# Output weights scaled and split in the x, B, C stage; that stage's raw weights fetched from ScalarE's queue

## The chip, the cores and the metric

The kernel runs on one core of a Trainium2 chip. The metric is the device time of one execution in microseconds (us), and lower is better. One execution of the kernel before was also recorded by the hardware profiler; the rows below come from that record. The engines are named PE (TensorE, matmul), DVE (VectorE), ACT (ScalarE), POOL (GpSimd) and SP (SyncE, which only issues DMAs here). ACT issues DMAs too, from a queue of its own.

## The reference

One layer of a diffusion backbone over 2048 latent tokens and 256 context tokens of width 1024. After an adaptive RMS norm, one wide projection feeds two mixers, and one output projection joins them:

```python
mod = silu(c) @ w_ada + b_ada                     # shift, scale, and the gate g of width 1024
p   = (rmsnorm(h, norm_w) * (1 + scale) + shift) @ w_in
u_pool, z_pool, z_ssd, xbc, dt = split(p)         # xbc: x, B and C of the state-space mixer
y_pool = (box means of u_pool - u_pool) @ pool_w * pool_scale * silu(z_pool)
y_ssd  = rmsnorm_by_group(ssd_bidirectional(silu(conv4(xbc)), dt) * silu(z_ssd), ssd_norm_w)
h      = h + g * (concat(y_pool, y_ssd) @ w_out)  # w_out: 2048 x 1024
out    = rmsnorm(h, final_norm_w)
```

The kernel does not multiply the output by g, pool_scale and the norm weight. It multiplies them into the 2048 rows and 1024 columns of w_out ahead of time: each raw row block of 128 rows is multiplied by `rowscale` (one number for each row) and by the gate (one number for each column). This preparation is what the change moves.

## The kernel before

**Split matmuls.** Every float32 operand is held as a high part, rounded to the format PE reads, and a low part, the rest. A product is hi*hi + hi*lo + lo*hi, so a 128x512 block of a projection over a depth of 1024 takes 24 matmuls. A raw weight tile (128x1024, 512 KB, tag `wraw`, a pool with two slots) is loaded by SP; ACT makes the high part by a CAST (L219), and POOL the low part by a subtraction (L220).

**Stages.** (1) Start, up to about 150 us: modulation, norm, and the first two column tiles of x. (2) The x, B, C stage, up to about 500 us: column tiles `ct` 2 to 15. Each has four blocks of 512 tokens, and those below 12 a context block too. A block is 24 matmuls; ACT copies the result out of PSUM (L315), POOL fills the edges of the copy (L317 to L323), DVE and ACT do the convolution of width 4 (L268 to L272), and the results go to DRAM. At the head of tile ct, `weights()` loads and splits the weights of tile ct + 1. (3) The sweep, 502 to 813 us: z and pool projections of the upper token blocks, and the backward state sweep, one chunk at a time. (4) The box stage, 813 to 1065 us: box means on DVE beside the projections of the lower blocks. (5) The ramp, 1065 to 1150 us: the first steps of the main loop in the hand-written order of the string `RAMP`. (6) The main loop, 1150 to 1690 us: 16 steps, each with scores, state, gate, norm and the output projection against the prepared `wout`.

**Who sets the order.** A tile scheduler orders the instructions of stages 1 to 4, by a simulated timeline; each engine then works strictly in its order. The ramp and the main loop stand as written.

**The gate and w_out before.** The gate row is summed in tiles 10 to 13 by `gate_row` (128x1024 multiplications on DVE) and stored to `s_gate`. In the sweep it is read back, and two matmuls with a matrix of ones spread it over all partitions into two PSUM tiles, `gb0` and `gb1`, of the tag `pp`. That tag has four banks, which the projections of sweep and box share, and gb0 and gb1 keep two of them until their last use in the ramp. Row blocks 8 to 15 of w_out are scaled in the sweep (`rescale`: two DVE instructions each) and stored raw to `s_wo`. `prepare(k)` then loads a raw block k (512 KB), scales it if k < 8, casts the high part on ACT (L846) and subtracts the low part on POOL or DVE (L851). It runs for k = 0 to 4 in the box stage and for 5 to 15 in the ramp, where the words `prep_load/5`, `prep_hi/5` and so on give each part its place.

Of the kernel before, what the change touches and what calls it, by code (L numbers as in the profile page):

```python
# [8 lines left out]
F32 = mybir.dt.float32  # L9
F32R = mybir.dt.float32r  # L10
AF = mybir.ActivationFunctionType
ALU = mybir.AluOpType
# [11 lines left out]
def hybrid_block(ctx, tc, d, out):  # L24
    nc = tc.nc
    P = 128
# [9 lines left out]
    def pp(name):  # L36
        return psum.tile([P, 512], F32, tag="pp", name=name)

    def aux(name):
        return psum.tile([P, 512], F32, tag="aux", name=name)  # L40

    def const(name, shape, src=None, dt=F32, pool=None):
        t = (pool or cpool).tile(shape, dt, tag=name, bufs=1, name=name)
        if src is not None:
            nc.sync.dma_start(t, src)
        return t

    def dram(name, shape):
        return drp.tile(shape, F32, tag=name, name=name)

    def mm(o, l, r, start, stop):
        nc.tensor.matmul(o, l, r, start=start, stop=stop)  # L52
# [9 lines left out]
    s_zp = dram("s_zp", [8, P, 1024])  # L62
    s_yp = dram("s_yp", [NCH, P, 8, P])
    s_af = dram("s_af", [P, 2, NC2, 16])
    s_gate = dram("s_gate", [P, 1024])
    s_wo = dram("s_wo", [8, P, 1024])
    s_rows = dram("s_rows", [2, NCH, 16, P])

    wstack = ExitStack()
# [1 line left out]
    rpool = rstack.enter_context(tc.tile_pool(name="rawp", bufs=2, side="right"))  # L71
    wpool = wstack.enter_context(tc.tile_pool(name="wpool", bufs=2, side="right"))
    dstack = ExitStack()
    dp = dstack.enter_context(tc.tile_pool(name="dtp", bufs=1, side="right"))
# [3 lines left out]
    sp = start.enter_context(tc.tile_pool(name="startp", bufs=2))  # L78
# [138 lines left out]
    def split_weights(raw, nm, eng=nc.gpsimd):  # L217
        w = wpool.tile([P, 2, 8, P], F32R, tag="w", name=f"w_{nm}")
        nc.scalar.copy(w[:, 0], raw)  # L219
        eng.tensor_tensor(w[:, 1], raw, w[:, 0].bitcast(F32), op=ALU.subtract)  # L220
        return w

    def weights(src, nm):

        return split_weights(raw_weights(src, nm), nm)
# [105 lines left out]

    hc = dp.tile([P, 2, 8, 256], F32R, tag="hc", name="hc")
    dt_raw = const("dt_raw", [P, NC2, 32], pool=dp)
    wd = dp.tile([P, 8, P], F32R, tag="wd", name="wd")
    ctxt = Tokens(hc, 256, d["ctxT"], 1, "c", wpool.tile([P, 8, 256], F32, tag="w", name="xc"))
    ada = [slot(f"ada{a}", [P, 4, 2048], F32) for a in range(2)]
    cu = slot("cu", [P, 8192], F32)
# [163 lines left out]
    tabs = ctx.enter_context(tc.tile_pool(name="tabs", bufs=1))  # L501
    triU = const("triU", [P, P], d["triU"], pool=tabs)
    triL = const("triL", [P, P], d["triL"], pool=tabs)
    n4 = [P, 2, NC2, 16]
    dt_t = const("dt_t", n4, pool=tabs)
    af_t = const("af_t", n4, pool=tabs)
# [55 lines left out]
    def gate_row(k):  # L562

        wg = rpool.tile([P, 1024], F32, tag="wraw", name=f"wg{k}")
        nc.sync.dma_start(wg, d["w_ada"][k * P:(k + 1) * P, 2048:3072])
        if k == 0:
            nc.vector.tensor_scalar(gacc, wg, scol[:, k, 0:1], None, op0=ALU.mult)
        else:
            nc.vector.scalar_tensor_tensor(gacc, wg, scol[:, k, 0:1], gacc, op0=ALU.mult, op1=ALU.add)
        if k == 7:  # L570
            brow = rpool.tile([1, 1024], F32, tag="wraw", name="brow")
            nc.sync.dma_start(brow, d["b_g"])
            nc.vector.tensor_tensor(gacc[0:1, :], gacc[0:1, :], brow, op=ALU.add)
            nc.scalar.dma_start(s_gate, gacc)

    late = [lambda c=c, b=b: c.recall(b) for c in cols[0:2] for b in (4, 0, 1, 2, 3)]
    tables = dt_tables()
# [1 line left out]
    for ct in range(2, 16):  # L579
        next(tables, None)  # L580
        col = cols[ct]
        col.w = wx.pop(ct)
        if ct < 15:
            wx[ct + 1] = weights(d["w_xbc"][ct + 1], f"x{ct + 1}")
        if ct < 12:
            col.context()
            col.context_out()
        for b in range(4):
            col.block(b)
            col.block_out(b)  # L590
            col.conv()
            if ct > 12 and late:
                late.pop(0)()
        if ct in (10, 11, 12, 13):
            for k in range(2):
                gate_row(2 * ct - 20 + k)
    gstack.close()
    cstack.close()
    dstack.close()
    tabs2 = ctx.enter_context(tc.tile_pool(name="tabs2", bufs=1))  # L600
    rowscale = const("rowscale", [P, 16], d["rowscale"], pool=tabs2)
    dskip = const("dskip", [P, 16], d["d_skip"].broadcast_to([P, 16]), pool=tabs2)
    allone = const("allone", [P, P], pool=tabs2)
    nc.vector.memset(allone, 1.0)
    mcol = const("mcol", [P, 1], pool=tabs2)
    nc.vector.memset(mcol, 1.0 / 256.0)
    hst = const("hst", [P, 4, 256], pool=tabs2)
# [102 lines left out]
    with tc.tile_pool(name="sweepp", bufs=2) as bp, tc.tile_pool(name="evp", bufs=3) as ep:  # L710
        sw, silus = sweep(bp), []
        count, taken = [0], [1]
        len_sweep, len_between = 74, 7 * 3 * 2 * 8

        def between():
            count[0] += 1
            if count[0] * len_sweep >= len_between * taken[0]:
                taken[0] += 1
                next(sw, None)

        def rescale(raw, k):

            for j in range(2):
                js = raw[:, 512 * j:512 * j + 512]
                nc.vector.scalar_tensor_tensor(js, js, rowscale[:, k:k + 1], gb[j], op0=ALU.mult, op1=ALU.mult)

        upper = (2, 3)
        for j in range(8):
            w = weights(d["w_z"][j], f"z{j}_2")
            for b in upper:  # L730
                silus.append(z_block(ep, w, j, b, between if j else None))
                if j == 0 and b == 2:
                    next(sw)
            if j == 1:
                gacc = rpool.tile([P, 1024], F32, tag="wraw", name="gacc2")
                nc.sync.dma_start(gacc, s_gate)
                gb = [pp(f"gb{j}") for j in range(2)]
                for j in range(2):
                    mm(gb[j], allone, gacc[:, 512 * j:512 * j + 512], True, True)
            for k in {1: (), 7: (5, 6, 7)}.get(j, (j - 2,) if j else ()):  # L740
                raw = rpool.tile([P, 1024], F32, tag="wraw", name=f"wos{k}")
                nc.sync.dma_start(raw, d["w_out"][1024 + k * P:1152 + k * P, :])
                rescale(raw, 8 + k)
                nc.scalar.dma_start(s_wo[k], raw)
            for src, dst, fn in ((d["w_zp"][j], s_zp, AF.Silu), (s_wp[j], s_v, AF.Copy)):
                w = weights(src, f"p{j}_{fn}")
                for i, b in enumerate(upper):
                    t = ep.tile([P, 512], F32, tag="ev", name=f"e{j}_{b}_{fn}")
                    ps = pp(f"pp{j}_{b}_{fn}")
                    project(ps, w, hm[b], between if j else None)  # L750
                    nc.scalar.activation(t, ps, fn)
                    nc.scalar.dma_start(dst[j, :, 512 * i:512 * i + 512], t)
        for _ in sw:
            pass
# [77 lines left out]
    bx = slot("bx", [P, 8192], F32)  # L832
    wout = [slot("wout0", [P, 4, 2, 1024], F32R)]

    raws = {}

    def prep_load(k):
        raws[k] = rpool.tile([P, 1024], F32, tag="wraw", name=f"wor{k}")
        nc.sync.dma_start(raws[k], s_wo[k - 8] if k >= 8 else d["w_out"][k * P:(k + 1) * P, :])

    def prep_scale(k):
        if k < 8:
            rescale(raws[k], k)

    def prep_hi(k):
        nc.scalar.copy(wout[k // 4][:, k % 4, 0, :], raws[k])  # L846

    def prep_lo(k, eng=None):
        wo = wout[k // 4][:, k % 4]
        eng = eng or (nc.gpsimd if k in (1,3,4,5,7,13,15) else nc.vector)  # L850
        eng.tensor_tensor(wo[:, 1, :], raws[k], wo[:, 0, :].bitcast(F32), op=ALU.subtract)  # L851

    def prepare(k):
        prep_load(k)
        prep_scale(k)
        prep_hi(k)
        prep_lo(k)

    with tc.tile_pool(name="boxp", bufs=1) as xp:
        for i, j in enumerate(order):  # L860
# [256 lines left out]
    for i in (4, 5):  # L1117
        w = following()
# [81 lines left out]
        wout.append(slot(f"wout{len(wout)}", [P, 4, 2, 1024], F32R))  # L1200

    kp = None
    other = {f.__name__: f for f in (prep_load, prep_scale, prep_hi, prep_lo, z, zg, logs, work, more)}

    RAMP = """
    0:load prep_load/5 1:load 0:scores 0:carried 0:shift 0:mask 0:exponents prep_scale/5 1:shift 0:steps_mix
    prep_hi/5 logs 0:decay z/6/0 1:scores 1:carried zg/6/0 z/7/0 0:mix 0:from_states prep_load/6 
    0:mix2 1:mask 1:exponents 2:load prep_scale/6 1:steps_mix prep_hi/6 1:decay zg/7/0 2:scores 2:carried more  # L1210
    1:from_states 1:mix 0:outputs z/6/1 prep_lo/5 prep_load/7 0:load_pool prep_lo/6
    0:gate 2:mask prep_scale/7 1:mix2 prep_load/8 1:load_pool 0:squares 2:shift
    2:steps_mix 0:square_sum 2:exponents 1:outputs 0:norm_mm z/7/1 more work prep_hi/8 prep_hi/7 zg/6/1 prep_lo/8
    0:state prep_lo/7 3:load 2:from_states 1:gate 0:pool_hi 1:squares zg/7/1 logs 0:norm1 
    1:square_sum 0:norm2/0 1:pool_hi 2:decay 2:mix 0:pool_lo 1:pool_lo 3:scores 1:norm_mm 0:out/0/0
    0:out/0/1 1:norm1 0:norm2/1 0:norm2/2 0:norm2/3 0:diag 0:spread 2:mix2 3:mask 2:outputs 1:out/0/0 0:scale 3:carried 1:out/0/1
    0:ssd_hi 3:shift 2:state 0:ssd_lo 1:state 2:gate 3:steps_mix 2:squares 2:square_sum 3:exponents 2:norm_mm
# [99 lines left out]
```

## Time and profile before

| | us |
|---|---|
| median of 3 runs | 1691.6 (1691.33 to 1699.04) |
| the profiled execution, its own time | 1691.25 |
| span of its trace, first to last instruction | 1689.5 |
| PE busy | 1626.3 (96% of the span) |
| DVE, ACT, POOL busy | 1209.4, 768.4, 599.5 |

The profiled execution took 1691.25 us, 1.75 us more than its span, and lies 0.35 us below the median. The granted TensorE clock was 0.983 of full speed over the whole span. PE is the engine with the least idle time, so a change is felt where PE waits, or where its clock falls.

### The profile page before, as it was taken

The page shows a single profiled execution, that of the slowest core. Times are in us where ns is not written, and L with a number is a line of the kernel's source. Part 1 is how long each engine was busy: PE and PEld are TensorE (multiplying, and loading weights), DVE is VectorE, ACT ScalarE, POOL GpSimd, SP SyncE. Part 2 cuts the span into 40 slices and gives each one's busy share as a digit, 9 for nine tenths or more (in the row PEclk, how much of TensorE's full clock was granted, in tenths as well). Part 3 has the DMA queues.
Part 4 walks back from the last instruction along what each step waited for, and adds up shares of the span by engine and source line. Part 5 has one row for each costly group of instructions (what it writes and reads, how often), then busy time and mean ns, then how long its engine had stood idle before and what let it go on. Part 6 is the DMA issues. An engine that isn't in the chain of part 4 may idle for free. (4 is left out here: it accounts for less than half of the span.)

```text
span 1689.5 us, 25001 instructions
## 1 busy us (share of the span) xinstructions
PE 1626.3 (96%) x7786; PEld 1306.6 (77%) x7786; DVE 1209.4 (72%) x2514; ACT 768.4 (45%) x1841; POOL 599.5 (35%) x667
## 2 busy tenths in 40 slices
PE   8889999999999999999999989869999999999997
PEld 6668888888887887787887868757888888888886
DVE  2575755566772888886199998547788888888885
ACT  5563453433453444443212122455565556555653
POOL 1231111111223667775433334323333333333331
PEclk9989999999999999999999999989999999999999
DMA  9823333466564678878624356675666667666762
GB/s 388 283 75 100 76 74 73 93 155 155 144 137 153 203 248 252 255 249 272 207 87 150 114 184 187 188 223 184 186 194 208 195 203 199 198 208 192 194 194 83
DMA packets 315543, 302.57 MB, mean 179 GB/s; under 512 B 132626, under 2 KB 244114, under 8 KB 312851
## 3 DMA queue, kind: packets, MB, share of 16 engines
q1 hardware_dynamic: 246594, 237.27, 48.9%
q10 hardware_dynamic: 68816, 63.71, 11.3%
q8 instruction: 61, 1.00, 0.2%
q14 instruction: 72, 0.58, 0.1%
HBM read 207.28 MB, written 93.62 MB: 178 GB/s over the span
## 5 line engine op out<-in xcount | busy, mean ns | idle before, releaser
L52 PE MATMUL px<-hm,w_x 128*128 128x512 f32 x1536 | 364.8, 397 | 2.7 <-ACT hm L205 2.4
L52 PEld LDWEIGHTS px<-hm,w_x 128*128 128x128 f32 x1536 | 288.0, 188 | 73.3 <-ACT hm L205 4.1
L52 PE MATMUL po<-wout,yp 128*128 128x512 f32 x768 | 213.0, 413 | 0.0
L52 PE MATMUL po<-wout,ys 128*128 128x512 f32 x768 | 211.0, 410 | 0.0
L52 PE MATMUL pz<-hm,w_z 128*128 128x512 f32 x768 | 188.9, 398 | 0.7 <-POOL w_z L220 0.7
L270 DVE SCALAR_TENSOR_TENSOR cacc<-u,conv_w,cacc 128x512 f32<-128x512 f32 x168 | 141.5, 854 | 66.3 <-POOL u L320 47.5
L52 PEld LDWEIGHTS pz<-hm,w_z 128*128 128x128 f32 x768 | 145.0, 189 | 36.0 <-POOL w_z L220 1.1
L52 PEld LDWEIGHTS po<-wout,yp 128*128 128x128 f32 x768 | 135.9, 190 | 34.7 <-issue 10.6
L52 PEld LDWEIGHTS po<-wout,ys 128*128 128x128 f32 x768 | 136.3, 190 | 23.7
L960 POOL TENSOR_TENSOR yp<-yl,yp 128x256 fp32r<-128x256 f32 x64 | 50.3, 786 | 229.2 <-ACT yp L956 220.8
L644 DVE TENSOR_TENSOR xw<-xt,w_t 128x256 f32<-128x256 f32 x144 | 99.3, 728 | 31.5 <-POOL xr L651 17.0
L651 POOL TENSOR_TENSOR xr<-xw,xh 128x512 fp32r<-128x512 f32 x72 | 99.7, 1387 | 27.4 <-ACT xh L649 27.4
L960 POOL TENSOR_TENSOR ys<-yg,ys 128x256 fp32r<-128x256 f32 x64 | 63.1, 986 | 116.9 <-ACT ys L956 66.6
L52 PE MATMUL ivationFunctionType.Copy<-hm,ivationFunctionType.Copy 128*128 128x512 f32 x384 | 97.7, 401 | 2.3 <-POOL ivationFunctionType.Copy L220 1.7
L52 PE MATMUL pv<-hm,w_v 128*128 128x512 f32 x384 | 92.9, 402 | 5.9 <-ACT zt L795 5.9
L52 PE MATMUL ivationFunctionType.Silu<-hm,ivationFunctionType.Silu 128*128 128x512 f32 x384 | 95.9, 396 | 0.0
L649 ACT CAST xh<-xw 128x512 fp32r<-128x512 f32 x72 | 44.7, 621 | 110.0 <-DVE xw L644 48.9
L52 PE MATMUL pzp<-hm,w_q 128*128 128x512 f32 x384 | 91.3, 396 | 1.2 <-ACT va L788 1.2
L52 PEld LDWEIGHTS pv<-hm,w_v 128*128 128x128 f32 x384 | 73.6, 192 | 24.1 <-ACT zt L795 6.3
L52 PEld LDWEIGHTS ivationFunctionType.Copy<-hm,ivationFunctionType.Copy 128*128 128x128 f32 x384 | 73.1, 191 | 20.5 <-POOL ivationFunctionType.Copy L220 2.1
L52 PEld LDWEIGHTS pzp<-hm,w_q 128*128 128x128 f32 x384 | 72.0, 188 | 19.2 <-ACT va L788 1.6
L904 ACT ACTIVATE e<-e,nrb_t 128x128 f32<-128x128 f32 x256 | 81.1, 388 | 12.2 <-DMA e<-s_rows 11.9
(269 smaller groups left out, 3046.3 us busy)
## 6 DMA issues: line engine op xcount, KB each, us to landing
e<-s_rows SPq DMA_DIRECT2D x128, 256.0 KB, 5.1
s_tok<-tkw ACTq DMA_DIRECT2D x64, 256.0 KB, 3.0
bc<-s_bc SPq DMA_DIRECT2D x64, 256.0 KB, 4.3
st<-s_tok SPq DMA_DIRECT2D x64, 256.0 KB, 5.5
xt<-s_xt SPq DMA_DIRECT2D x72, 128.0 KB, 3.4
ada<-in_w_ada_dram SPq DMA_DIRECT2D x8, 1024.0 KB, 15.7
wraw_x<-in_w_xbc_dram SPq DMA_DIRECT2D x16, 512.0 KB, 4.4
s_bc<-cacc ACTq DMA_DIRECT2D x32, 256.0 KB, 3.2
```

What stands on the lines that cost most here:

```text
L52: nc.tensor.matmul(o, l, r, start=start, stop=stop)
L270: nc.vector.scalar_tensor_tensor(acc, u[:, k:k + n], conv_w[:, ct, k:k + 1], acc, op0=ALU.mult, op1=ALU.add)
L644: nc.vector.tensor_tensor(xw[:, s], h4(xt), w_t[:, s, c, 4 * g:4 * g + 4].unsqueeze(2).broadcast_to([P, 4, 64]), op=ALU.mult)
L649: nc.scalar.copy(xh, xw)
L651: nc.gpsimd.tensor_tensor(xr, xw, xh.bitcast(F32), op=ALU.subtract)
L904: nc.scalar.activation(s.e2[:, h, :], s.e2[:, h, :], AF.Identity, bias=nrb_t[:, s.c, 4 * s.g + h:4 * s.g + h + 1])
L960: nc.gpsimd.tensor_tensor(y[:, 1], src, y[:, 0].bitcast(F32), op=ALU.subtract)
```

## The change

The gate is now summed in tiles 3 to 6. Its last `gate_row` spreads it at once, through a PSUM tile of another tag, and ACT copies it back to SBUF, into `gacc`; `s_gate`, gb0 and gb1 are gone. A new function `prep(k)` is called once behind each block of tiles 8 to 11, 16 times in all. It loads the raw block k on SP (the same two `wraw` slots as the x weights use), scales it by halves of 512 columns on DVE, casts the high part of a half on ACT into a tile `wo` (one slot), subtracts the low part on POOL, and stores the half, 512 KB, on SP into a larger `s_wo`. `prepare(k)` has become one load of 1 MB. The raw weights of the next x tile are now fetched from ACT's queue instead of SP's. The steps of the preparation leave sweep, box and ramp; `rowscale` and the ones are made earlier; `wd`, 4 KB a partition, moves to another pool.

```diff
-    s_gate = dram("s_gate", [P, 1024])
-    s_wo = dram("s_wo", [8, P, 1024])
+    s_wo = dram("s_wo", [16, P, 2, 1024])
...
-            nc.scalar.dma_start(s_gate, gacc)
+            for j in range(2):
+                gb = aux(f"gb{j}")
+                mm(gb, allone, gacc[:, 512 * j:512 * j + 512], True, True)
+                nc.scalar.copy(gacc[:, 512 * j:512 * j + 512], gb)
+
+    def prep(k):
+
+        raw = rpool.tile([P, 1024], F32, tag="wraw", name=f"wos{k}")
+        nc.sync.dma_start(raw, d["w_out"][k * P:(k + 1) * P, :])
+        for j in range(2):
+            js = slice(512 * j, 512 * j + 512)
+            nc.vector.scalar_tensor_tensor(raw[:, js], raw[:, js], rowscale[:, k:k + 1], gacc[:, js],
+                                           op0=ALU.mult, op1=ALU.mult)
+            w = gp.tile([P, 2, 512], F32R, tag="wo", bufs=1, name=f"wo{k}_{j}")
+            nc.scalar.copy(w[:, 0], raw[:, js])
+            nc.gpsimd.tensor_tensor(w[:, 1], raw[:, js], w[:, 0].bitcast(F32), op=ALU.subtract)
+            nc.sync.dma_start(s_wo[k, :, :, js], w.bitcast(F32))
...
-            wx[ct + 1] = weights(d["w_xbc"][ct + 1], f"x{ct + 1}")
+            raw = rpool.tile([P, 8, P], F32, tag="wraw", name=f"wraw_x{ct + 1}")
+            nc.scalar.dma_start(raw, d["w_xbc"][ct + 1])
+            wx[ct + 1] = split_weights(raw, f"x{ct + 1}")
...
             col.conv()
+            if 8 <= ct < 12:
+                prep(4 * ct - 32 + b)
...
-        if ct in (10, 11, 12, 13):
+        if 3 <= ct < 7:
             for k in range(2):
-                gate_row(2 * ct - 20 + k)
+                gate_row(2 * ct - 6 + k)
...
     def prepare(k):
-        prep_load(k)
-        prep_scale(k)
-        prep_hi(k)
-        prep_lo(k)
+        nc.sync.dma_start(wout[k // 4][:, k % 4].bitcast(F32), s_wo[k])
...
-    0:load prep_load/5 1:load 0:scores 0:carried 0:shift 0:mask 0:exponents prep_scale/5 1:shift 0:steps_mix
+    0:load prepare/5 1:load 0:scores 0:carried 0:shift 0:mask 0:exponents 1:shift 0:steps_mix
```

ACT's order between column tiles 10 and 12, before. A name ends in a number that only tells tiles apart; `px11_3` is block 3 of tile 11, `u11_3` its copy, `cacc` the convolution, `w_x12` the split weights of tile 12:

```order
L315 COPY u10_2_3042<-px10_2_3017 128x512
L268 ACTIVATE cacc_10_8_3088<-u10_2_3042,conv_b_156,conv_w_154 128x512
L272 ACTIVATE cacc_10_4_3046<-cacc_10_4_3046 128x512
L262 DMA s_bc_69<-cacc_10_4_3046 128x4x128
L315 COPY u10_3_3083<-px10_3_3058 128x512
L219 CAST w_x12_3120<-wraw_x12_3118 128x1024
L268 ACTIVATE cacc_10_12_3100<-u10_3_3083,conv_b_156,conv_w_154 128x512
L272 ACTIVATE cacc_10_8_3088<-cacc_10_8_3088 128x512
L306 COPY uc11_3148<-pc11_3123 128x256
```

The same engine now, at the end of tile 11. `wo9_1` is the second half of row block 9; line numbers have moved by one (L314 for L315, L218 for L219), L590 is the new CAST and L603 the fetch of the raw x weights:

```order
L590 CAST wo9_1_3169<-wos9_3161 128x512
L314 COPY u11_3_3509<-px11_3_3484 128x512
L267 ACTIVATE cacc_11_12_3526<-u11_3_3509,conv_b_155,conv_w_153 128x512
L271 ACTIVATE cacc_11_8_3514<-cacc_11_8_3514 128x512
L261 DMA s_bc_69<-cacc_11_8_3514 128x4x128
L590 CAST wo10_0_3217<-wos10_3214 128x512
L271 ACTIVATE cacc_11_12_3526<-cacc_11_12_3526 128x512
L261 DMA s_bc_69<-cacc_11_12_3526 128x4x128
L590 CAST wo10_1_3222<-wos10_3214 128x512
L603 DMA wraw_x12_3292<-in_w_xbc_dram 128x1024
L590 CAST wo11_0_3283<-wos11_3280 128x512
L218 CAST w_x12_3294<-wraw_x12_3292 128x1024
```

The CAST of w_x12 has moved from the end of tile 10 to behind the last copy of tile 11, behind three more halves of w_out and behind the fetch of its raw tile. At the next tile boundary the order is alike: the copy of `u12_3` and the halves 12_1 to 14_1 stand ahead of the fetch of `wraw_x13`, and 15_0 behind it, ahead of the CAST of w_x13.

SP's order in the ramp, before (`wor` is a raw block of w_out, `yl`, `bc`, `e`, `tk` and `st` are inputs of the steps):

```order
L839 DMA wor7_9122<-in_w_out_dram 128x1024
L893 DMA yl0_0_9124<-s_yp_74 128x256
L839 DMA wor8_9135<-s_wo_77 128x1024
L893 DMA yl0_1_9137<-s_yp_74 128x256
L880 DMA bc0_3_9206<-s_bc_69 128x512
```

The same place now (a `wout` is the prepared tile of four row blocks):

```order
L838 DMA wout1_8912<-s_wo_76 128x2048
L874 DMA yl0_0_9239<-s_yp_74 128x256
L838 DMA wout2_9195<-s_wo_76 128x2048
L874 DMA yl0_1_9248<-s_yp_74 128x256
L838 DMA wout2_9195<-s_wo_76 128x2048 x3
L861 DMA bc0_3_9313<-s_bc_69 128x512
```

Five loads of 1 MB stand where two of 512 KB stood, and the inputs of the next steps are issued behind them.

## Rows read from the trace of the kernel before

**Rows 1.** The page: busy time of each engine; PE's granted clock in 40 slices.

```profile
PE 1626.3 (96%) x7786; PEld 1306.6 (77%) x7786; DVE 1209.4 (72%) x2514; ACT 768.4 (45%) x1841; POOL 599.5 (35%) x667
PEclk9989999999999999999999999989999999999999
```

**Rows 2.** Stretches: length, busy PE, PEld, DVE, ACT, POOL; clock, DMA share, GB/s.

```profile
200.00:502.00 302.00, 302.00 (x1390) 247.62 (x1390) 195.74 (x269) 136.48 (x209) 53.15 (x130) 1.00 0.54 117
502.00:813.00 311.00, 305.04 (x1286) 242.65 (x1285) 222.03 (x371) 128.21 (x280) 193.25 (x156) 0.99 0.73 233
813.00:1065.00 252.00, 244.95 (x1041) 196.38 (x1040) 205.06 (x79) 50.51 (x72) 94.97 (x59) 0.99 0.47 146
1065.00:1150.00 85.00, 64.43 (x292) 50.22 (x290) 44.08 (x104) 45.27 (x92) 26.93 (x21) 0.88 0.72 218
1150.00:1690.00 540.00, 530.63 (x2938) 429.71 (x2938) 428.65 (x1498) 308.92 (x996) 187.37 (x234) 1.00 0.64 188
376.78:402.00 25.22, 25.22 (x121) 20.91 (x120) 16.57 (x22) 9.65 (x16) 3.48 (x9) 1.00 0.68 149
0.00:50.00 50.00, 41.57 (x208) 29.00 (x208) 9.48 (x29) 24.46 (x63) 10.79 (x16) 1.00 0.97 385
```

**Rows 3.** PE's waits: line and what it waited for; us, times, longest.

```profile
PE yo L52 <- DMA st<-s_tok: 6.8, 1, 6.8
PE pv L52 <- ACT zt L795: 5.9, 1, 5.9
```

**Rows 4.** PE's timeline in the x, B, C stage: start, us, operation, count.

```profile
351.51 3.04 PE L52 MATMUL pc<-hc,w_x 128*128 128x256 f32 x24
354.39 22.55 PE L52 MATMUL px<-hm,w_x 128*128 128x512 f32 x96
376.78 3.04 PE L52 MATMUL pc<-hc,w_x 128*128 128x256 f32 x24
```

**Rows 5.** Timeline of all engines, 345 to 362 us, in column tile 10.

```profile
347.40 0.59 ACT L315 COPY u<-px 128x512 f32<-128x512 f32 x1 [0.57 <-ACT cacc L272]
348.05 0.19 POOL L320 COPY u<-u 128x1 f32<-128x1 f32 x1 [6.33 <-ACT u L315]
...
349.20 1.54 DVE L270 SCALAR_TENSOR_TENSOR cacc<-u,conv_w,cacc 128x512 f32<-128x512 f32 x2 [0.17 <-ACT cacc L268]
...
352.20 1.05 ACT L219 CAST w_x<-wraw_x 128x1024 fp32r<-128x1024 f32 x1
...
353.86 2.40 POOL L220 TENSOR_TENSOR w_x<-wraw_x,w_x 128x1024 fp32r<-128x1024 f32 x1
353.94 3.52 DVE L270 SCALAR_TENSOR_TENSOR cacc<-u,conv_w,cacc 128x512 f32<-128x512 f32 x2 [2.58 <-POOL u L320]
```

**Rows 6.** Groups of like instructions: busy us, mean ns of one; scaling: min/median/max.

```profile
L220 POOL TENSOR_TENSOR w_x<-wraw_x,w_x 128x1024 fp32r<-128x1024 f32 x12 | 29.6, 2470 | 7.0 <-ACT w_x L219 5.4 <-DMA s_bt<-u 0.8 <-DMA s_xt<-u 0.8
L651 POOL TENSOR_TENSOR xr<-xw,xh 128x512 fp32r<-128x512 f32 x72 | 99.7, 1387 | 27.4 <-ACT xh L649 27.4
L649 ACT CAST xh<-xw 128x512 fp32r<-128x512 f32 x72 | 44.7, 621 | 110.0 <-DVE xw L644 48.9
...
L725 DVE SCALAR_TENSOR_TENSOR wos<-wos,rowscale,gb x16: 733/742/750, 550.6 to 776.9; 128x512 f32<-128x512 f32 x16
```

**Rows 7.** DMAs: size of each, median us from issue to landing.

```profile
s_wo<-wos ACTq DMA_DIRECT2D x8, 512.0 KB, 3.2
...
wraw_x<-in_w_xbc_dram SPq DMA_DIRECT2D x10, 512.0 KB, 4.3
s_gate<-gacc ACTq DMA_DIRECT2D x1, 512.0 KB, 5.1
```

**Rows 8.** Groups of the preparation in the ramp, 1065 to 1150 us.

```profile
L846 ACT CAST wout<-wor 128x1024 fp32r<-128x1024 f32 x12 | 12.4, 1044 | 19.3 <-DMA wor<-s_wo 10.9 <-DVE zt L828 7.1 <-DVE wor L725 1.3
L851 POOL TENSOR_TENSOR wout<-wor,wout 128x1024 fp32r<-128x1024 f32 x5 | 12.2, 2446 | 30.9 <-ACT wout L846 30.9
```

**Rows 9.** Stretches of 5 us in the ramp; columns as in rows 2.

```profile
1100.00:1105.00 5.00, 3.59 (x17) 2.80 (x18) 0.17 (x1) 1.38 (x2) 0.00 (x0) 0.55 0.89 328
1140.00:1145.00 5.00, 2.71 (x8) 2.34 (x9) 4.36 (x18) 2.84 (x10) 1.86 (x3) 0.50 0.31 105
```

More of the change, by code (lines that the diff above doesn't have):

```diff
@@ L333, in hybrid_block @@
     dt_raw = const("dt_raw", [P, NC2, 32], pool=dp)
-    wd = dp.tile([P, 8, P], F32R, tag="wd", name="wd")
+    wd = sp.tile([P, 8, P], F32R, tag="wd", bufs=1, name="wd")
     ctxt = Tokens(hc, 256, d["ctxT"], 1, "c", wpool.tile([P, 8, 256], F32, tag="w", name="xc"))
@@ L503, in hybrid_block @@
     triL = const("triL", [P, P], d["triL"], pool=tabs)
+    rowscale = const("rowscale", [P, 16], d["rowscale"], pool=tabs)
+    allone = const("allone", [P, P], pool=tabs)
+    nc.vector.memset(allone, 1.0)
     n4 = [P, 2, NC2, 16]
@@ L600, in hybrid_block @@
     tabs2 = ctx.enter_context(tc.tile_pool(name="tabs2", bufs=1))
-    rowscale = const("rowscale", [P, 16], d["rowscale"], pool=tabs2)
     dskip = const("dskip", [P, 16], d["d_skip"].broadcast_to([P, 16]), pool=tabs2)
-    allone = const("allone", [P, P], pool=tabs2)
-    nc.vector.memset(allone, 1.0)
     mcol = const("mcol", [P, 1], pool=tabs2)
@@ L719, in between @@
                 next(sw, None)
[L721 to L725, printed above, removed]
         upper = (2, 3)
@@ L733, in hybrid_block @@
                     next(sw)
[L734 to L744, printed above, removed]
             for src, dst, fn in ((d["w_zp"][j], s_zp, AF.Silu), (s_wp[j], s_v, AF.Copy)):
@@ L833, in hybrid_block @@
     wout = [slot("wout0", [P, 4, 2, 1024], F32R)]
[L835 to L851, printed above, removed]
     def prepare(k):
-        prep_load(k)
-        prep_scale(k)
-        prep_hi(k)
-        prep_lo(k)
+        nc.sync.dma_start(wout[k // 4][:, k % 4].bitcast(F32), s_wo[k])
     with tc.tile_pool(name="boxp", bufs=1) as xp:
@@ L1202, in hybrid_block @@
     kp = None
-    other = {f.__name__: f for f in (prep_load, prep_scale, prep_hi, prep_lo, z, zg, logs, work, more)}
+    other = {f.__name__: f for f in (prepare, z, zg, logs, work, more)}
     RAMP = """
-    0:load prep_load/5 1:load 0:scores 0:carried 0:shift 0:mask 0:exponents prep_scale/5 1:shift 0:steps_mix
[L1209 to L1214, printed above, removed]
+    0:load prepare/5 1:load 0:scores 0:carried 0:shift 0:mask 0:exponents 1:shift 0:steps_mix
+    logs 0:decay z/6/0 1:scores 1:carried zg/6/0 z/7/0 0:mix 0:from_states prepare/6
+    0:mix2 1:mask 1:exponents 2:load 1:steps_mix 1:decay zg/7/0 2:scores 2:carried more
+    1:from_states 1:mix 0:outputs z/6/1 prepare/7 0:load_pool
+    0:gate 2:mask 1:mix2 prepare/8 1:load_pool 0:squares 2:shift
+    2:steps_mix 0:square_sum 2:exponents 1:outputs 0:norm_mm z/7/1 more work zg/6/1
+    0:state 3:load 2:from_states 1:gate 0:pool_hi 1:squares zg/7/1 logs 0:norm1
     1:square_sum 0:norm2/0 1:pool_hi 2:decay 2:mix 0:pool_lo 1:pool_lo 3:scores 1:norm_mm 0:out/0/0
```

## The prediction

> **What bounds the kernel now.** I read the page's busy times first: PE is busy for 1626.3 of 1689.5 us, no other engine over 1209.4, and its clock is full except at the start and in one slice near two thirds of the span [rows 1]. So only PE's idle time and that slice can be won, and every wait put before PE is lost. The windows by stage place this [rows 2]: in the x, B, C stage PE is busy for 302.0 of 302.0 us at clock 1.00, so nothing can be won there; sweep and box leave 6.0 and 7.1 us idle; the ramp leaves 85.0 − 64.4 = 20.6 us and has a clock of 0.88, which costs about 64.4 × 0.12 = 7.7 us more. The list of PE's waits shows the single ones [rows 3], and the timelines give the pace of the x, B, C stage [rows 4, 5].
>
> The change takes work from the stages with gaps and puts it into the one without. It is cheap there by busy time: ACT is busy for 136, DVE for 196 and POOL for 53 of 302 us [rows 2]. What decides is the order in which it stands, and what each piece waits for.
>
> **The new chain of halves.** The tile `wo` has one slot, so the CAST of a half must wait until the store of the half before has landed, and POOL's subtraction must lie between. The 32 halves are strictly serial. One period P is a CAST of 128x512, 0.62 us; a subtraction of 128x512, 1.39 in another place, or 1.24 as half of 2.47 for 128x1024 [rows 6]; a store of 512 KB from issue to landing; and the hand-overs, of which ACT to POOL took 0.06 (347.40 + 0.59 to 348.05) [rows 5], say 0.25 for all. This store isn't in the trace. Transfers of the same size took 3.2 (s_wo, in the sweep), 4.3 (the raw x weights, in this stage) and 5.1 us (s_gate, in this stage) [rows 7]. So P lies between 0.62 + 1.24 + 3.2 + 0.2 = 5.3 and 0.62 + 1.39 + 5.1 + 0.3 = 7.4. I take the 4.3 of this stage: 0.62 + 1.31 + 4.3 + 0.25 = **6.5 us**. The bytes themselves fit: 8 MB of loads and 16 MB of stores over some 225 us add about 107 GB/s to 149, against 385 GB/s in the first 50 us [rows 2].
>
> **Where PE waits for it.** Before, the CAST of w_x12 stood at the end of tile 10, a whole tile of 25.3 us (351.51 to 376.78) ahead of PE's need [rows 4]. Now ACT's order around it is: wo9_1, the last copy of tile 11, wo10_0, wo10_1, the fetch of wraw_x12, wo11_0, the CAST of w_x12. The fetch must find a free `wraw` slot, that of block 10, so it waits for POOL's half 10_1; ACT works in order, so everything behind it waits too.
>
> *Stall at tile 12.* wo9_1 stands ahead of the copy of the last block, about half a block (2.8 us) before PE ends tile 11. Two periods later comes wo10_1, then CAST and POOL (0.62 + 1.24 + 0.2 = 2.1), the load (4.3) and the CAST of w_x12 (1.05) [rows 5, 7]. PE waits 2P − 2.8 + 2.1 + 4.3 + 1.05 = 2P + 4.65: 17.7 us at P = 6.5; 15.3 and 19.5 at the ends.
>
> *Stall at tile 13.* The fetch of wraw_x13 stands behind 14_1, eight halves after 10_1, by the same path. Meanwhile PE has only the four blocks of tile 12, 354.39 to 376.78 = 22.4 us in tile 10 [rows 4]. It waits 8P − 22.4: 29.6 us; 20.0 and 36.8 at the ends. Behind it only block 15 is left, and tiles 14 and 15 find their raw weights in time.
>
> *Lag in tiles 7 to 11.* Here about one half stands behind each block copy on ACT, 20 in all, while a block with its share of the context comes every 25.3 / 4 = 6.3 us. Where P is longer, ACT's copies fall behind and PE waits for PSUM: 20 × (6.5 − 6.3) = 4.0 us; 0 and 22.0 at the ends.
>
> Together 51.3 us (35.3 to 78.3). To this comes the clock behind two long waits: a stretch of 5 us in the ramp that was partly idle ran at 0.55 [rows 9], which costs 2.25 us, so 4.5 for two. The additions in tiles 3 to 6 (the gate multiplications come earlier, two small matmuls) lie beside a DVE with 106 us free [rows 2] and I put them at 0.
>
> **What is won.** *Ramp:* 12 CASTs of 1.04 us, five subtractions of 2.45 us on POOL [rows 8] and others on DVE, and the scalings of 0.74 [rows 6] go; ACT's CASTs waited 10.9 us for raw loads [rows 8]. Ends: 0, if PE's gaps are those of the steps' own inputs, and 20.6 + 7.7 = 28.3, all idle time and all lost clock. One gap of 6.8 us is for `st`, an input from s_tok [rows 3], and there are others without the preparation (at 1140 DVE was busy for 4.36 of 5 us and PE for 2.71) [rows 9]. I take half, 14. The loads grow: a prepared block is 1 MB, and SP issues the next steps' inputs behind them; what is late next is therefore an input. *Box:* the wait of 5.9 us of pv for ACT's zt [rows 3] came with two PSUM banks of four; with four, and without the preparation of blocks 0 to 4, I take 6 (0 to 7.1). *Sweep:* 16 scalings of 0.74 us [rows 6] go, mostly beside PE: 1 (0 to 6.0). Together −21 (0 to −41.4).
>
> **Sum.** +51.3 + 4.5 − 21 = +34.8. The profiled execution took 1691.25 us (0.35 below the median of 1691.6), so 1691.25 + 34.8 = 1726. With every term at its end: 35.3 + 4.5 − 41.4 = −1.6 (1690), and 78.3 + 4.5 = +82.8 (1774).
>
> **Rivals.** *A, not slower (12%).* The stores land in 3.2 us or less, so that P is 5.3, and the ramp and box, rid of the preparation, give back all their idle time and clock: −1.6, that is 1690. For it: s_wo stores took 3.2 at a DMA share of 0.73, higher than here [rows 2, 7], and CASTs in the ramp waited for raw loads. Against it: the ramp's own inputs. It turns at the point where the gains exceed 2P + 4.65 + 8P − 22.4 + 4.5, which is 39.8 at P = 5.3: the ramp alone, with 28.3, can't do it.
>
> *B, POOL and DVE in each other's way (20%).* While POOL made the low half of w_x (353.86, 2.40 us), the pair of convolution instructions on DVE took 3.52 us instead of 1.54 [rows 5]. The new scaling and the convolution share the stage with 32 more subtractions. If each of those waits once for a convolution instruction, 1.54 / 2 = 0.77 us, P is 7.3: 19.3 + 36.0 + 20.0 = 75.3, and 75.3 + 4.5 − 21 = +58.8: 1750. Against it: such a collision needs both at once, and DVE is busy for only 65% of the stage [rows 2].
> The Trainium skill, page "SBUF — State Buffer", section "Who interferes with whom", says that a DVE instruction with two SBUF inputs contends with a GpSimd instruction that reads SBUF, since its second input comes through the shared read interface; the scaling now reads both gacc and the raw block from SBUF, where before it read the gate from PSUM. The stretch of 3.52 us agrees with that rule, which speaks for this rival and against the change. By the rule the sum would be this rival's, without it the forecast's.
>
> *C, the ramp gains nothing (15%).* Five loads of 1 MB stand on SP ahead of bc0_3 and the inputs behind it, where two of 512 KB stood. At the 328 GB/s of the busiest stretch [rows 9] a block of 1 MB takes 3.2 us, five 16, against 3.2 for the two: 12.8 us in which inputs queue, as much as I credit. Then 51.3 + 4.5 − 7 = +48.8: 1740. For it: the DMA share is already 0.72, and 0.89 in the stretch [rows 2, 9].
>
> **How the numbers follow.** The forecast has 53% and an own range of 1708 to 1744 (P from 6.0 to 7.0 moves the sum from 42.3 to 66.3, and the gain in the ramp by some 7 either way). With A at 1690, C at 1740 and B at 1750, a range of 1698 to 1762 leaves out most of A and the upper end of B. About 0.5%, 8.5 us, is what a measurement of this kernel tells from no change. Faster needs A with still shorter stores: 5%. Within 0.5%: the rest of A and a little of the forecast's lower end, 9%. Slower: 86%.
>
> **What would show it.** Right: in the new trace PE waits about 18 us ahead of the first matmul of tile 12 and about 30 ahead of tile 13, for ACT's CAST of w_x, at L218; the CASTs of `wo` stand 6 to 7 us apart from tile 7 to 13, each right behind a landed store; the x, B, C stage ends some 50 us later, and box and ramp take back some 20. B shows as subtractions or CASTs of `wo` delayed with DVE's convolution beside them; C as PE in the ramp waiting for inputs on SP. Wrong: PE without a gap at tile 12 and 13, a period near or below 5, or halves in flight two at a time; then the stage costs little and the gains in box and ramp decide.

## The result, and the profile after

The changed kernel takes 1730.74 us (median of 4 runs, 1727.32 to 1732.63) against 1691.46 us before: a ratio of 1.0233, 95% interval 1.0208 to 1.0258. It is slower by about 39 us; the forecast was 1726. The profiled execution has a span of 1729.5 us, 40.0 more than before.

The page of the changed kernel, busy times and PE's granted clock in 40 slices:

```profile
PE 1626.9 (94%) x7786; PEld 1308.0 (76%) x7786; DVE 1208.1 (70%) x2505; ACT 772.4 (45%) x1859; POOL 630.5 (36%) x692
PEclk9999999998789999999999999999999999999999
```

PE does the same 7786 matmuls in nearly the same busy time as in [rows 1] (1626.9 against 1626.3), so over the whole span the 40 us are idle time of PE. A new dip of the clock stands in the tenth to twelfth slice, the x, B, C stage. To compare stage by stage, both traces are cut at the same events: the start of tile 7, the first matmul of the sweep, the first of the box stage, the last z product, and a fixed matmul group of the first step. The columns are those of [rows 2]. Before:

```profile
275.71:491.65 215.94, 215.94 (x986) 176.68 (x984) 144.02 (x193) 94.94 (x148) 38.21 (x94) 1.00 0.58 131
491.65:834.30 342.65, 336.69 (x1421) 268.14 (x1420) 231.02 (x383) 138.67 (x298) 206.38 (x168) 0.99 0.72 230
834.30:1056.77 222.47, 215.42 (x914) 172.60 (x912) 196.17 (x72) 44.41 (x61) 81.30 (x49) 0.98 0.46 142
1056.77:1145.67 88.90, 68.56 (x301) 53.83 (x300) 47.96 (x93) 43.95 (x85) 29.75 (x20) 0.88 0.67 201
```

The same stretches of the changed kernel:

```profile
275.88:552.52 276.64, 224.51 (x989) 181.92 (x988) 150.78 (x207) 109.92 (x175) 79.11 (x123) 0.90 0.66 174
552.52:887.80 335.28, 330.48 (x1417) 265.58 (x1416) 241.17 (x374) 143.80 (x304) 208.39 (x171) 1.00 0.67 214
887.80:1102.18 214.38, 213.36 (x914) 171.24 (x913) 189.30 (x63) 40.33 (x57) 78.21 (x47) 1.00 0.47 151
1102.18:1185.38 83.20, 68.93 (x301) 54.40 (x300) 27.05 (x76) 31.99 (x72) 18.05 (x16) 0.92 0.87 291
```

The x, B, C stage has grown by 60.7 us: 52.1 us in which PE is idle (276.64 − 224.51), and 8.6 us of longer busy time. That is the lower clock (0.90 over the stage) and the two products that spread the gate (four records in the trace, 1.88 us). The sweep gives back 7.4, the box stage 8.1, the ramp 5.7: 21.2 in all. The main loop is the same within 0.3.

PE's list of waits says for what it is idle (line, what it waited for; us, times, longest):

```profile
PE px L52 <- ACT w_x L218: 43.1, 2, 23.0
PE pc L52 <- ACT w_x L218: 9.0, 1, 9.0
...
PE yo L52 <- DMA st<-s_tok: 7.6, 2, 5.1
PE n L52 <- ACT dg L995: 6.1, 2, 4.4
```

Three waits for the CAST of w_x, 52.1 us together, are all of it. PE's timeline shows where they lie; the number in brackets is the idle time ahead of the row:

```profile
387.87 0.79 PE L52 MATMUL pc<-hc,w_x 128*128 128x256 f32 x2 [9.04 <-ACT w_x L218]
...
394.10 21.16 PE L52 MATMUL px<-hm,w_x 128*128 128x512 f32 x90
438.23 24.92 PE L52 MATMUL px<-hm,w_x 128*128 128x512 f32 x96 [22.97 <-ACT w_x L218]
483.27 69.42 PE L52 MATMUL px<-hm,w_x 128*128 128x512 f32 x288 [20.12 <-ACT w_x L218]
```

They stand ahead of tiles 11, 12 and 13. The 96 matmuls of tile 12 took 24.92 us instead of the 22.55 of [rows 4]: the granted clock was 0.90 over these 24.92 us, and 1.00 in the stage before the change. ACT's timeline ahead of tile 12 shows the chain at work:

```profile
428.66 0.62 ACT L590 CAST wo<-wos 128x512 fp32r<-128x512 f32 x1 [5.17 <-DMA s_wo<-wo]
430.64 0.37 ACTq L603 DMA_DIRECT2D wraw_x<-in_w_xbc_dram  x1
436.61 0.62 ACT L590 CAST wo<-wos 128x512 fp32r<-128x512 f32 x1 [7.34 <-DMA s_wo<-wo]
437.14 1.04 ACT L218 CAST w_x<-wraw_x 128x1024 fp32r<-128x1024 f32 x1
```

The first CAST is half 10_1. It waited 5.17 us for the store of the half before. Only behind its subtraction can the raw tile of tile 12 be fetched (430.64), and the CAST of that tile stands behind one more half, 11_0, which waited 7.34 us for the store of 10_1. The fetch itself had landed by then, 4.6 us after its issue. PE starts 1.1 us after the CAST of w_x begins. The halves as a group (ns min/median/max, first and last start; then ACT's idle time ahead of these CASTs that a store ended, us and times):

```profile
L590 ACT CAST wo<-wos x32: 606/619/624, 285.2 to 486.8; 128x512 fp32r<-128x512 f32 x32
L591 POOL TENSOR_TENSOR wo<-wos,wo x32: 1262/1289/1691, 285.9 to 487.4; 128x512 fp32r<-128x512 f32 x32
...
  DMA s_wo<-wo: 78.7, 26
...
DMA to landing us min/median/max: 3.0/3.6/6.4
```

From half 0_0 (285.17) to 10_1 (428.66) there are 21 periods, 6.83 us each on average; from 10_1 to 14_1 (473.89) there are eight of 5.65. Of these eight, the one that holds the fetch of the raw tile took 7.95 us (428.66 to 436.61), the seven others 5.0 to 5.7. The fetch and the store of 10_1 were issued together, at 430.64, and that store took 5.9 us to land instead of the usual 3.6; the three other stores that were issued within 0.2 us of such a fetch, and whose landing is on record, took 6.4, 6.0 and 5.7. SP, too, issues in its order, and in the first 21 periods some stores came late. The longest delay is 4.1 us, from the end of a subtraction (313.47 + 1.43) to its store:

```profile
313.47 1.43 POOL L591 TENSOR_TENSOR wo<-wos,wo 128x512 fp32r<-128x512 f32 x1 [5.50 <-DMA s_xt<-u]
...
318.98 0.52 SPq L592 DMA_DIRECT2D s_wo<-wo  x1
```

### The profile page after: what moved, and what is told of

Read it like the earlier page. It is cut to its first block, busy times and chain, and to the rows that moved or that the text cites. A ratio compares the mean times of both kernels' runs of the same rounds, so it can differ in the third digit from the quotient of the medians.

```text
span 1729.5 us, 25085 instructions
## 1 busy us (share of the span) xinstructions
PE 1626.9 (94%) x7786; PEld 1308.0 (76%) x7786; DVE 1208.1 (70%) x2505; ACT 772.4 (45%) x1859; POOL 630.5 (36%) x692
## 4 chain that ended last, share of the span: by engine, by line
PE 55%; DMA 9%; DVE 7%; POOL 2%; issue 2%; ACT 2%; SPq 1%; ACTq 0%; DVEq 0%; POOLq 0%
PE po L52 21%; PE pz L52 6%; PE ivationFunctionType.Copy L52 5%; PE ivationFunctionType.Silu L52 5%; DMA s_wo<-wo 4%; PE pv L52 4%; PE yo L52 3%; PE st L52 3%; PE pzp L52 3%; PE y L954 2%; PE y L960 2%; DVE bx L823 2%; DVE bx L813 2%; DVE cacc L269 1%; PE n L52 1%
## 5 line engine op out<-in xcount | busy, mean ns | idle before, releaser
L52 PE MATMUL px<-hm,w_x 128*128 128x512 f32 x1536 | 371.4, 401 | 45.9 <-ACT w_x L218 43.1
L52 PEld LDWEIGHTS px<-hm,w_x 128*128 128x128 f32 x1536 | 291.9, 191 | 118.5 <-ACT w_x L218 44.0
L52 PEld LDWEIGHTS po<-wout,yp 128*128 128x128 f32 x768 | 136.2, 190 | 34.7 <-issue 10.6
L591 POOL TENSOR_TENSOR wo<-wos,wo 128x512 fp32r<-128x512 f32 x32 | 42.0, 1311 | 132.5 <-ACT wo L590 121.2
L52 PEld LDWEIGHTS ivationFunctionType.Silu<-hm,ivationFunctionType.Silu 128*128 128x128 f32 x384 | 72.0, 188 | 21.1 <-POOL ivationFunctionType.Silu L219 2.7
```

What stands on the lines that cost most here:

```text
L591: nc.gpsimd.tensor_tensor(w[:, 1], raw[:, js], w[:, 0].bitcast(F32), op=ALU.subtract)
```

## The experiments

Each kernel was timed side by side with the kernel before; ratios are to that, with 95% intervals. Three things make the theory: the halves are serial, their raw blocks share two slots with the x weights, and four blocks a tile ask for more than the chain can do.

**Only block 0 prepared in the stage.** This takes nearly all of the preparation away and leaves the rest of the change.

```diff
-                prep(4 * ct - 32 + b)
+                if ct == 8 and b == 0:
+                    prep(0)
...
-.bitcast(F32), s_wo[k])
+.bitcast(F32), s_wo[0])
```

> The changed kernel, but only row block 0 of w_out is prepared in the x, B, C stage; blocks 1 to 15 are left out there, and every later load reads block 0 (same bytes, wrong values). Theory (the cost is the serial chain of halves and the x weights behind it): no wait of PE at tiles 11 to 13 (52.1 us of waits and some 7 us of clock go), so 1666 to 1676 us, and sweep, box and ramp keep their gain of about 21. Rival (the cost is the earlier gate, the moved queue or the clock alone): 1700 us or more.

Measured: 1667.03 us, ratio 0.9858 (0.9837 to 0.9880). The stretch from tile 7 on and the sweep:

```profile
275.00:493.67 218.67, 218.67 (x995) 178.26 (x993) 137.33 (x189) 98.63 (x154) 39.87 (x98) 1.00 0.53 118
493.67:823.20 329.53, 329.53 (x1417) 265.84 (x1416) 228.81 (x362) 138.32 (x296) 205.86 (x166) 1.00 0.67 215
```

PE has no idle time in either. The earlier gate and the moved queue cost nothing beyond the 2.0 us by which the sweep starts later than before (493.67 against 491.65), in which the gate's two matmuls lie. The whole loss comes with the preparation of the 15 other blocks, and the gain without it is some 22 to 24 us (22 by the medians, against 1689.46 for the kernel before, and 24 by the ratio).

**The raw x weights from SP's queue again.**

```diff
-            nc.scalar.dma_start(raw, d["w_xbc"][ct + 1])
-            wx[ct + 1] = split_weights(raw, f"x{ct + 1}")
+            wx[ct + 1] = weights(d["w_xbc"][ct + 1], f"x{ct + 1}")
```

> The changed kernel with the raw x weights fetched from SP's queue again. Theory (the x weights wait for a raw slot that a block of w_out holds, on whichever queue): 1722 to 1738 us, PE's waits for w_x still 45 to 60 us. Rival (the fetch is late because it stands in ACT's queue behind CASTs that wait): waits for w_x of at most 25 us, about 1700 us.

Measured: 1718.28 us, ratio 1.0159 (1.0137 to 1.0181), a little below the range of the theory. The waits remain:

```profile
PE px L52 <- ACT w_x L218: 39.3, 2, 20.8
...
PE pc L52 <- ACT w_x L218: 6.6, 1, 6.6
```

45.9 us instead of 52.1, and the sweep is 5.7 us shorter than in the changed kernel (329.6). So of the 12 us about half are won in the waits for w_x (6.2) and half in the sweep. The queue is a smaller part of the loss; most of the waits stay on either one.

**A raw slot of their own for the x weights.** The gate stays in PSUM, to make room.

```diff
-            raw = rpool.tile([P, 8, P], F32, tag="wraw", name=f"wraw_x{ct + 1}")
+            raw = gp.tile([P, 8, P], F32, tag="xraw", bufs=1, name=f"wraw_x{ct + 1}")
...
-            nc.vector.scalar_tensor_tensor(raw[:, js], raw[:, js], rowscale[:, k:k + 1], gacc[:, js],
+            nc.vector.scalar_tensor_tensor(raw[:, js], raw[:, js], rowscale[:, k:k + 1], gb[j],
```

> The changed kernel with one raw slot of their own for the x weights; to make room the spread gate stays in two PSUM tiles instead of going back to SBUF. The halves are as serial as before. Theory (shared slot is the coupling): no gap at tiles 12 and 13; what is left is ACT in order behind CASTs that wait, 10 to 30 us, so 1680 to 1705 us. Rival (ACT's order alone makes the waits): 1715 us or more.

Measured: 1683.75 us, ratio 0.9967 (0.9948 to 0.9986). The halves are as serial as before (from 278.3 to 483.0, 6.6 us each), but the waits for w_x are gone; what PE waits for is ACT. The first row is a weight tile of the z_pool projection, early in the sweep; the profile cuts its name:

```profile
PE ivationFunctionType.Silu L52 <- ACT ivationFunctionType.Silu L218: 6.4, 1, 6.4
...
PE px L52 <- ACT u L314: 3.3, 3, 2.1
```

**Two slots for the halves**, raw slots shared as in the change, the gate in PSUM.

```diff
-            w = gp.tile([P, 2, 512], F32R, tag="wo", bufs=1, name=f"wo{k}_{j}")
+            w = gp.tile([P, 2, 512], F32R, tag="wo", bufs=2, name=f"wo{k}_{j}")
```

> The changed kernel with two slots for the halves (tile wo); to make room the spread gate stays in PSUM. Raw slots are shared as in the changed kernel. Theory (the chain store-CAST-subtraction is the cost): two halves in flight, a period of 3.5 to 4.5 us, so 8P - 22.4 is 6 to 14 us and the wait at tile 12 goes: 1675 to 1695 us. Rival (transfers or DVE and POOL are the limit): a period of 5.5 us or more, 1715 us or more.

Measured: 1684.07 us, ratio 0.9962 (0.9950 to 0.9974). The 32 halves now run from 288.5 to 441.1, 4.9 us each, slower than expected, and one wait is left, at tile 13:

```profile
442.68 69.49 PE L52 MATMUL px<-hm,w_x 128*128 128x512 f32 x288 [13.94 <-ACT w_x L218]
```

Undoing either half of the coupling, the shared slot or the serial chain, wins back the whole loss of 39 us and some 6 us more. So the loss needs both; these two runs and the next control show it.

**The gate in PSUM alone.** The two runs before also keep the gate in PSUM, so this was tried by itself.

> The changed kernel with the spread gate left in two PSUM tiles instead of copied back to SBUF, and nothing else changed: it separates this part of the runs with an own slot and with two slots. Theory (it doesn't matter): 1726 to 1736 us. Rival (a scaling that reads two inputs from SBUF holds POOL up): periods shorter by 0.5 us or more, 1720 us or less.

Measured: 1734.18 us, ratio 1.0274 (1.0260 to 1.0288), with waits for w_x of 56.7 us (42.8 + 13.9). The subtractions took as long as with the gate in SBUF (median 1292 ns against 1289). It wins nothing, so the gain of the two runs is that of the slots.

**Two blocks a tile**, over tiles 8 to 15, everything else as in the change.

```diff
-            if 8 <= ct < 12:
-                prep(4 * ct - 32 + b)
+            if ct >= 8 and b % 2 == 0:
+                prep(2 * ct - 16 + b // 2)
```

> The changed kernel with two row blocks a tile over tiles 8 to 15 instead of four over 8 to 11; halves stay serial, raw slots shared, gate in SBUF. Theory (four blocks a tile ask for 8 periods of 5.6 to 6.8 us in a tile of 25.3, so the queue of halves pushes the x weights back; four periods fit): no wait of over 5 us for w_x, 1672 to 1690 us. Rival (any half ahead of a fetch costs): waits of 20 us or more remain, 1695 us or more.

Measured: 1702.23 us, ratio 1.0098 (1.0085 to 1.0111), outside the theory's range and inside the rival's. The waits for w_x are gone, as it said, but the serial halves now last until 531.9, and the same thing happens to the sweep's first weights:

```profile
PE pz L52 <- ACT w_z L218: 17.7, 1, 17.7
PE px L52 <- ACT u L314: 9.6, 4, 5.1
```

**Two slots and two blocks a tile.**

> The kernel of the run with two slots for the halves, with two row blocks a tile over tiles 8 to 15. Theory: the x, B, C stage is free of waits, and the time is that of the run with only block 0 prepared (1667.0), within 5 us: 1664 to 1673. Rival (the 15 other blocks cost PE through DMA or ACT even when nothing is serial): 1678 us or more.

Measured: 1687.20 us, ratio 1.0006 (0.9997 to 1.0016). The time is in the rival's range. Two halves are in flight and no w_x is waited for, yet 20 us of the gain are missing. They are missing in two places, from tile 7 to the sweep's start and in the sweep:

```profile
274.50:505.40 230.90, 223.31 (x994) 180.27 (x994) 162.07 (x201) 106.22 (x170) 81.81 (x121) 0.99 0.76 205
505.40:843.10 337.70, 332.28 (x1417) 267.69 (x1416) 240.55 (x381) 145.60 (x307) 208.57 (x173) 0.99 0.67 216
```

These are 12.2 and 8.2 us longer than the two rows of the run with only block 0; the stages behind are 3 us shorter. In the first, PE is idle for 7.6 us, nearly all of it waiting for ACT's copies (7.5). The convolutions run late: from 500 to 530 us DVE is still busy for 24.5 of 30 us, against 7.4 in that run, and there PE waits 3.3 and 2.1 us for the weights of z_pool, at a clock that falls to 0.66 from 520 to 530 us. Ahead of that, the late convolutions of tiles 0 and 1 (`ur`), which stand in tiles 13 to 15, are slow (those before 500 us):

```profile
L269 DVE SCALAR_TENSOR_TENSOR cacc<-ur,conv_w,cacc 128x512 f32<-128x512 f32 x12 | 15.6, 1299 | 0.7 <-ACT cacc L267 0.7
```

The mean is 1299 ns for these 12, and 1023 for all 24, against 746 in the run with only block 0. In the timeline the longest takes 2.86 us while a subtraction runs on POOL:

```profile
471.57 2.86 DVE L269 SCALAR_TENSOR_TENSOR cacc<-ur,conv_w,cacc 128x512 f32<-128x512 f32 x1
```

```profile
470.99 2.89 POOL L219 TENSOR_TENSOR w_x<-wraw_x,w_x 128x1024 fp32r<-128x1024 f32 x1
```

This subtraction is that of w_x, which the kernel before has too; what the preparation adds are the halves, and beside one of them (468.73 to 470.43) a convolution took 1.78 us (from 469.21).

**Quarters with an own slot.** Pieces of 256 columns, two in flight, x weights with their own slot, all prepared by tile 12, ahead of those late convolutions.

```diff
-            w = gp.tile([P, 2, 512], F32R, tag="wo", bufs=1, name=f"wo{k}_{j}")
+            w = wop[0].tile([P, 2, 256], F32R, tag="wo", bufs=2, name=f"wo{k}_{j}")
```

> The changed kernel with a raw slot of their own for the x weights and pieces of 256 columns instead of 512 (256 KB a store), two in flight; the sum of the gate is given up behind tile 6 to make room, the gate stays in PSUM. Four blocks a tile as in the changed kernel, so that all is prepared by tile 12. Theory (serial pieces and the shared slot were the whole cost): no wait of PE for w_x, the time of the run with only block 0 prepared (1667.0) plus at most 8 us: 1666 to 1676. Rival (the preparation costs PE in this stage anyway, through DVE and POOL in each other's way, as the run with two slots and two blocks a tile, 1687.2, suggests): 1680 us or more.

Measured: 1688.73 us, ratio 1.0001 (0.9989 to 1.0014). The rival again, but not by its reason alone: the late convolutions are less disturbed (781 ns for the 14 before 500 us, 856 for all 24), and ACT waits, in its own order:

```profile
L593 ACT CAST wo<-wos 128x256 fp32r<-128x256 f32 x64 | 25.7, 404 | 67.2 <-DMA s_wo<-wo 62.1 <-DVE wos L588 2.3 <-DVE cacc L269 1.6
```

Of the 67.2 us for which ACT was idle ahead of these CASTs, stores ended 62.1, and the copies of PE's results stand behind them. One such place, with a wait of 2.75 us on PE's side:

```profile
394.31 0.40 ACT L593 CAST wo<-wos 128x256 fp32r<-128x256 f32 x1 [5.55 <-DMA s_wo<-wo]
394.94 0.41 ACT L593 CAST wo<-wos 128x256 fp32r<-128x256 f32 x1 [0.22 <-DMA s_wo<-wo]
395.25 0.58 ACT L314 COPY u<-px 128x512 f32<-128x512 f32 x1
```

```profile
395.89 40.98 PE L52 MATMUL px<-hm,w_x 128*128 128x512 f32 x168 [2.75 <-ACT u L314]
```

**The same with the fetch on SP.**

> The same as the run with quarters and a slot of their own, with the raw x weights fetched from SP's queue. Theory (with its own slot the fetch stands behind nothing that waits long): within 4 us of it. Rival (ACT's queue costs by itself, as 12 us did between the changed kernel and its run with the fetch on SP): 6 to 12 us faster.

Measured: 1686.87 us, ratio 0.9987 (0.9978 to 0.9997): within 4 us, as the theory has it. In these runs ACT's queue matters while the fetch stands behind something that waits long; the 2 us left are hardly clear of the noise.

**Two PSUM banks held.** The first try, on the kernel with two slots and two blocks a tile:

> The kernel with two slots for the halves and two blocks a tile, in which two of the four PSUM banks are taken in the sweep (two memsets on DVE) and given back behind the box stage, as the gate held them before. Theory (the gain of some 15 us in sweep and box comes from the banks): 8 to 16 us slower than without, most of it in the box stage. Rival (it comes from the scaling, splitting and loads that left these stages): within 3 us.

Measured: 1685.10 us, ratio 0.9990 (0.9979 to 1.0001). It tells nothing: the copies that give the banks back ran at 551 us, as soon as they could. The second try, on the kernel with quarters, gives them back with additions that read the last box mean:

```diff
+                held_banks = [pp(f"gh{i}") for i in range(2)]
...
+        nc.vector.tensor_tensor(mcol2, t[:, 0:1], bx[:, 3072 * n:3072 * n + 1], op=ALU.add)
```

> The kernel with quarters and an own slot, in which two of the four PSUM banks are taken in the sweep and given back by additions that read the last box mean, so at the end of the box stage. (In the earlier run with banks held the copies that gave them back were done at once, 4 us later.) Theory (the gain in sweep and box comes from the banks): 8 to 16 us slower than without. Rival (it comes from the scaling, splitting and loads that left): within 3 us.

Measured: 1686.85 us, ratio 0.9986 (0.9974 to 0.9999), not slower than the 1688.73 of the same kernel without. Here the banks were held until 1039.9 and 1061.8, near the end of the stage:

```profile
L757 DVE MEMSET gh<- x2: 485/485/485, 547.3 to 551.8; 128x512 f32 x2
L864 DVE TENSOR_TENSOR mcol<-gh,bx x2: 149/154/160, 1039.9 to 1061.8; 128x1 f32<-128x1 f32 x2
```

From its first matmul to the ramp's first, the box stage took 236.8 us in both (244.9 before). The gain there is not from these two banks.

**Half the bytes in the ramp.** On the kernel with two slots and two blocks a tile.

```diff
+            nc.sync.dma_start(wout[k // 4][:, k % 4, 0].bitcast(F32), s_wo[k, :, 0])
+            nc.gpsimd.memset(wout[k // 4][:, k % 4, 1].bitcast(F32), 0.0)
```

> The kernel with two slots for the halves and two blocks a tile; of row blocks 5 to 15 the ramp loads only the high half (512 KB instead of 1 MB), and POOL fills the low half with zeros, so that part of the output projection is left out. Theory (the ramp's waits left are for the steps' own inputs, which SP issues when their slots come free): within 3 us of the kernel with whole loads. Rival (the loads of 1 MB hold these inputs up): 4 to 9 us faster, PE's waits for st gone.

Measured: 1688.30 us, ratio 1.0008 (0.9993 to 1.0024), against 1687.20 with whole loads. The loads of the ramp landed in 6.6 us instead of 9.8, and PE's wait for `st` did not shrink (7.4 us with whole loads):

```profile
PE yo L52 <- DMA st<-s_tok: 14.0, 2, 9.3
```

So it is not the size of the loads that the ramp waits for. The number of loads ahead of the inputs on SP stayed the same, and POOL's fills came on top; no run tells what these two do.

## Why the prediction was right, and where its terms were not

The time (1726 against 1730.74), its sign and the mechanism were right: a serial chain of halves, x weights behind it, waits of PE at tile boundaries, and part of it given back later. The measured terms give 52.1 + 8.6 − 21.2 = 39.5 where 51.3 + 4.5 − 21 = 34.8 was forecast. That the waits (52.1 against 51.3) and the gains (21.2 against 21) agree so well is luck: their parts were off by 2 to 10 us in both directions, and cancel. The own range of the forecast, 1708 to 1744, doesn't follow from the swings named beside it, which add up to 1710 and 1748.

*The period.* Forecast 6.5 us. It was 6.83 up to half 10_1 and 5.65 behind it. The median store landed in 3.6 us, where 4.3 was taken, but single ones took 3.0 to 6.4, a wider spread than that of [rows 7] (3.2 to 5.1), and SP issued some late. Both lengthened the chain; ACT seldom did, for 26 of the 32 CASTs started out of an idle time that a store ended.

*The stalls.* At tile 13 the formula 8P − 22.4 stands: with 5.65, and with the 24.9 us that tile 12 took at the lower clock, 45.2 − 24.9 = 20.3, measured 20.1; forecast 29.6, since the store was put at 4.3 in P, and tile 12 at 22.4. At tile 12, 23.0 against 17.7: half 9_1 came at 416.21, when PE had already ended tile 11 (394.10 + 21.16 = 415.26), not 2.8 us before. That makes 3.75 us. From half 10_1 on the formula counted its CAST and subtraction, the load of the raw tile and the CAST of w_x, 7.45 us. But the CAST of 11_0, which stands ahead of that of w_x, came later than the load: it waited for one more store, the one beside the fetch. From 428.66 to PE's start at 438.23 it took 9.6 us, 2.1 more. The two periods between took 12.5 us instead of 13. The lag of tiles 7 to 11 was put at 4.0, as waits for PSUM. With P = 6.83 the same formula gives 20 × 0.53 = 10.6; 9.0 were measured, but in one piece, as a wait for w_x at tile 11. The mechanism of tiles 12 and 13 began a tile earlier than forecast. The clock and the gate's matmuls cost 8.6, where 4.5 was put for the clock and 0 for the matmuls.

*Sweep: the term outside its own bounds.* Forecast 1, outside its own ends of 0 to 6.0, measured 7.4. Those ends counted idle time alone. Idle time fell by 1.2 us (5.96 to 4.80); PE's busy time fell by 6.2 (336.7 to 330.5), of which the gate's four records moved to the x, B, C stage and the rest goes with a clock of 1.00 instead of 0.99. More was to be had: with only block 0 prepared the sweep took 329.5 us with no idle time, 13.1 less than before.

*Box.* Forecast 6, measured 8.1. Of the two reasons given, the two more PSUM banks fell with the held banks. What remains is the scaling and splitting of blocks 0 to 4 that left DVE and ACT; no run takes that apart further.

*Ramp.* Forecast 14, measured 5.7. PE's idle time there went from 20.3 to 14.3 us (stretches above), and the two waits left, 7.6 for st and 6.1 for dg, are for an input and for an intermediate of the steps themselves. Both stood in the trace before, at 6.8 [rows 3] and 8.9. Half of all idle time and lost clock was too generous an estimate.

*Rivals.* A (not slower) didn't happen. C (the ramp gains nothing) is half seen: the ramp gained 5.7 of 14, and PE waits there for an input, which is C's sign. But C's reason, the bytes of the 1 MB loads, was tried and doesn't hold. B's price didn't show in the changed kernel, where POOL's subtraction took 1.29 us (median); but DVE's side of it is seen in the run with two slots and two blocks a tile. The page "SBUF — State Buffer" of the Trainium skill, section "Who interferes with whom", says that a DVE instruction with two SBUF inputs contends with a GpSimd instruction that reads SBUF. The convolution of 2.86 us beside POOL's 2.89 agrees with that. Taking the gate from PSUM, which spares the scaling its second SBUF input, did not make the kernel faster (1734.18), so the scaling's part in it, if any, cost nothing here.

*What stays open.* With no wait for w_x left, the preparation still costs about 20 us against the run with only block 0 (1687 to 1689 against 1667.0). In the run with quarters, too, it lies in the x, B, C stage (230.7 us against 218.7) and in the sweep (339.5 against 329.5). ACT's waits for stores and DVE beside POOL are both seen in the rows; no run separates their shares, nor shows that they are all of it. The fastest whole kernels are those with an own slot and with two slots, 0.3 to 0.4% faster than before.

## What to carry to other kernels

Work that fits an idle engine by its busy time can still stop the engine that bounds the kernel: follow one piece through its slot, its store and the in-order engine, and compare that period with the pace at which the pieces are asked for. A tile with one slot that ends in a DMA makes every later piece wait for the landing, and what shares its raw slots or its engine waits too. Here a slot of its own for the one, or two slots for the other, each won back the loss, so either is the first thing to try; leaving the piece out shows what the most is that can be won.

## What the runs showed beside the question

A copy that is meant to hold a buffer can be moved to where it is ready: the banks were given back 4 us after they were taken. It takes an input that comes late to hold something. And what a queue costs depended on what stood ahead in it: moving the fetch of the x weights from ACT's to SP's queue was worth about 12 us with the shared slot, and 2 with an own one.
